# Three edits in a hybrid decoder step: mLSTM row operations at the second GLA value, SSD dt columns through one PSUM bank on ScalarE, urgent state updates, and a new step table

## The chip, the cores and the metric

The kernel runs on one core of a Trainium2 chip. The metric is the device time of one execution in microseconds (us); a measurement is the median over runs. The engines are TensorE (PE in the profile; its weight loads are PEld), VectorE (DVE), ScalarE (ACT), GpSimd (POOL) and SyncE (SP); each works through its own queue in order, and semaphores join them.

## The reference

One inference step of a small decoder trunk with two layers, for 512 prompt tokens and 8 samples of 4 tokens each (544 columns), model width 1024, all float32:

```python
for l in range(DEPTH):                      # DEPTH = 2
    if l % 2 == 0:                          # "AB": mLSTM heads and GLA heads
        mix, c, n, m, s = _ab_mixer(x, ...) # one input projection, 4 + 4 heads, one output projection
    else:                                   # "SSD": Mamba-2, 4 groups of 8 heads, causal conv of width 4
        mix, h, cv = _ssd_mixer(x, ...)
    x = _layernorm(DN_ALPHA * x + mix, ...)
    x = _layernorm(DN_ALPHA * x + _mlp(x, w1, w2), ...)   # squared ReLU, 4096 wide
```

In the mLSTM the gates give rows per head over the tokens: lf = log_sigmoid(f), its running sum b, and the running maximum m of b + (i - b), from which come the weights exp(D - m) of the scores. In the SSD, dt = softplus(dt_raw + bias), cs is the running sum of -exp(a_log) * dt in a chunk, and each group computes

```python
w = jnp.exp(seg) * dt                                  # seg[t, s] = cs[t] - cs[s], causal
y = einsum(CB, w, x) + einsum(C, h0) * exp(cs)
h = exp(cs_last) * h0 + einsum(exp(cs_last - cs) * dt, x, B)
```

for the prompt from a zero state, and for each sample from its given state. All new states are outputs.

## The kernel before

The work is in four stages: AB, MLP 0, SSD, MLP 1. Activations stand with features on the partitions, so a tile has 128 features x 272 columns (half of the 544; hf is the half). Each float32 weight tile is split on the chip into a high part whi (ScalarE, L167) and a rest wlo (VectorE, L168), and each product is three matmuls (xh by whi, xl by whi, xh by wlo; L378, L395, L590). These dense matmuls are the bulk of TensorE's work.

Everything else is fitted in between. Each of these side works (a GLA or mLSTM head, a group of the SSD, a LayerNorm) is a Python generator in a lane. `tick()` is called ahead of each dense matmul, and a lane whose count is used up goes on one step; `yield W["..."]` says how many dense matmuls are to pass until then, and `yield from need(key)` waits until another lane has set a key. So the table W fixes where TensorE's side instructions stand. A place in the program is given below as a tick: the number of dense matmuls ahead of it. The instructions of the other engines are put in order at build time by a scheduler, by when they could start in its model; code under `tc.high_priority()` is put ahead of what else is ready, and `tc.issue_after` (in `hold`) keeps operations behind a given one. On the chip each engine then follows its order strictly.

What the change touches:

- AB: `gla_scores` (L1050 to L1128) makes the scores of the GLA pairs q = 0 and 1 in levels: F = exp(A differences) on ScalarE, zq and zk on VectorE (L1092, L1094), gs on TensorE (L1102), a masked copy into sT (L1106). At its end "gscores" is set. `gla_heads` (L1390) runs the heads; ("g", n) is set when so many heads have given their values. A head ends in mean and variance (L873, L874), hf, hb and hn (L879 to L897).
- `ml_gates` (L1216): the mLSTM's rows on 4 partitions. First batch L1226 to L1237 (three passes on ScalarE, two scans and four passes on VectorE), second batch L1241 to L1258 behind head 2, then TensorE transposes uw into columns (uwt, L1280) and makes sample columns (sc, L1288).
- mLSTM heads: `ml_head` (row_bc's rowbc L769, md L1321, the outputs), pipelined with `W["mr"]` ticks between rounds (L1408); samples' products snum and supd (L969, L1008), for which GpSimd makes vm (L1004). When the heads are done, `then()` issues the loads of xf (L325) on GpSimd's queue.
- SSD: dt's rows (cs, dt, dw) are made on 32 partitions, written to DRAM for broadcast reads, and `dt_cols` (L1558) transposes them into two PSUM tiles rt and rt2, from which VectorE copies cols, ncs = -cs and csp. Each of four `group`s waits for "dt": transposes of B (Btp, Bts) and x (xt), the product cb, then per block of 128 tokens state, scores, outputs, each `W["sx"]` ticks on. E is loaded from DRAM, masked on GpSimd (L1666), exponentiated with ncs as bias (L1672), multiplied by cb (L1673). Then `samples`: four times `W["sq"]` ticks, products it (L1759) and sps (L1766), and eight updates h * dec + sp on VectorE (L1772), and after `W["so"]` ticks the output. All PSUM tiles by `pm` share a few banks, so a new one waits until the last reader of an older one is done.
- SSD's conv of the 24 tiles of x, B and C runs on ScalarE (L1604, L1609) and VectorE (L1606, L1611, L1612) as they come from the projection.
- `layernorm` (L455): sum over features (mu), squares, `W["v0"]` ticks later (first half; "v1" for the second, "vs" behind the SSD) their sum (var, L469), lnr, and xh and xl (L481, L482, L478) for the next stage.

Of the kernel before, what the change touches and what calls it, by code (L numbers as in the profile page):

```python
# [13 lines left out]
ALU = mybir.AluOpType  # L14
# [3 lines left out]
P = 128  # L18
D = 1024
KT = 8  # L20
NP = 512
NB, LS = 8, 4
NS = NB * LS
# [9 lines left out]
HEADM = 6  # L33
HEADA = 2

W = dict(dec=12, gates=30, gr=8, sc=16, lev=16, v=24, kd=10, out=48, hd=6, s0=42, ss=40, end=12, c0=20, u=13, s=16, ml=12, mr=52, dt=238, sg=72, sx=14, sq=26, so=48, l0=12, l1=12, v0=74, v1=55, f0=16, f1=18, f2=4, ls=20, vs=47)
GATES = ((0, 0, 4), (32, 4, 4), (64, 8, 16))
LEVELS = (64, 32, 16, 8, 4, 2, 1)

# [189 lines left out]
def trunk_kernel(ctx, tc, a, stages=("ab", "mlp0", "ssd", "mlp1")):  # L229
    nc = tc.nc  # L230
    V, S, G, TE = nc.vector, nc.scalar, nc.gpsimd, nc.tensor
# [6 lines left out]
    def pm(name):  # L238
        turn[0] += 1
        k = spare[0] and turn[0] % 5 == 0  # L240
        return psm.tile([P, 512], F32, tag="k" if k else "m", name=name, bufs=1 if k else 4)
# [10 lines left out]
    for st in stages:  # L252
# [10 lines left out]
        else:  # L263
# [3 lines left out]
            for kind, m, *r in MLP:  # L267
                if kind == "pair":
                    ws.plan(st, "pair", a["mlp_w1"][l, m], a["mlp_w1"][l, m + 1])
                else:  # L270
                    k, n = m % 8, r[0]
# [61 lines left out]
    def need(*keys):  # L333
        while not ready.issuperset(keys):
            yield 0
# [380 lines left out]
    def ab(pool, early, then):  # L716
# [11 lines left out]
        ident = C("ident")  # L728
# [486 lines left out]
        ml = {}  # L1215

        def ml_gates():
            rw = early.tile([P, T], F32, name="rw", bufs=1)
            uw = early.tile([P, T], F32, name="uw", bufs=1)
            z, t, b, u = rw[0:4], rw[32:36], rw[64:68], uw[0:4]  # L1220
            G.memset(uw, 0.0)
            S.copy(z, gate[32:36])
            S.copy(u, gate[0:4])
            yield from need("gscores")
            with hold("head"):
                S.activation(t, z, AF.Abs)  # L1226
                S.activation(t, t, AF.Exp, scale=-1.0)
# [11 lines left out]
            with hold("head"):  # L1239
                m = b  # L1240
# [37 lines left out]
            p = pm("uwt")  # L1278
            for b_ in range(4):
                TE.transpose(p[:, b_ * P:(b_ + 1) * P], uw[:, b_ * P:(b_ + 1) * P], ident)  # L1280
            cols = pool.tile([P, 4, 68], F32, name="cols", bufs=1)
# [4 lines left out]
            p = pm("sc")  # L1286
# [180 lines left out]
    def ssd(pool, ypool, dram, right, ahead, consts):  # L1467
# [7 lines left out]
        ident, smask, seqm, seye = C("ident"), C("smask"), C("seqm"), C("seye")  # L1475
# [81 lines left out]

        def dt_cols():  # L1558
            yield W["dt"]
            p1, p2 = pm("rt"), pm("rt2")  # L1560
            for b in range(4):
                TE.transpose(p1[:, b * 96:(b + 1) * 96], rows[:96, b * P:(b + 1) * P], ident[:96, :96])
            TE.transpose(p2[:NS, :96], rows[:96, NP:], ident[:96, :96])
            for o, b, q in ((slice(0, P), slice(0, 4), p1[:, :384].rearrange("p (b c) -> p b c", b=4)),
                            (slice(0, NS), slice(4, 5), p2[:NS, None, :96])):
                V.tensor_copy(cols[o, b], q[:, :, 32:])
                V.tensor_scalar(ncs[o, b], q[:, :, :32], -1.0, None, ALU.mult)
            V.tensor_copy(csp, p2[:NS, :32])
            for r in (64, 96):
                S.activation(ecs[r:r + NS], ncs[:NS, 4], AF.Exp, scale=-1.0)  # L1570
            ready.add("dt")
# [171 lines left out]
        def samples(g, X, outputs, z, Bs, Xs):  # L1743

            heads = slice(8 * g, 8 * g + 8)
            it = psm.tile([P, 512], F32, tag="k", name="it", bufs=1)
            for q in range(0, NB, 2):
                h0 = [pool.tile([P, 512], F32, tag="h0", name="h0", bufs=4) for _ in range(2)]
                for k in range(2):
                    nc.sync.dma_start(out=h0[k], in_=a["h0"][g, q + k])  # L1750
                hn = pool.tile([P, 2, 512], F32, tag="h0n", name="h0n", bufs=2)
                nc.sync.dma_start(out=hn, in_=a["h0n"][g, q // 2])
                Bm = pool.tile([96, 2, P], F32R, tag="Bm", name="Bm", bufs=2)
                for k in range(2):
                    S.activation(Bm[:, k], Bs.bitcast(F32), AF.Identity, scale=seqm[:96, q + k:q + k + 1])
                yield W["sq"]

                for k in range(2):
                    TE.matmul(it[64 + NS * k:64 + NS * k + NS], Cm[:, NS * (q + k):NS * (q + k) + NS], h0[k],  # L1759
                              start=q == 0, stop=q == NB - 2)  # L1760
                for i in range(2):
                    sp = pm("sps")
                    spv = sp.rearrange("p (j k n) -> p j k n", j=2, k=2)
                    for j in range(2):
                        m = 2 * i + j
                        TE.matmul(sp[:, 256 * j:256 * j + 256], Xs[:, m * P:(m + 1) * P], Bm.rearrange("p k n -> p (k n)"),  # L1766
                                  start=True, stop=True)
                    for j in range(2):
                        m = 2 * i + j
                        for k in range(2):  # L1770
                            h = hn[:, k, m * P:(m + 1) * P]
                            V.scalar_tensor_tensor(h, h, decs[:, 4 * g + m, q + k:q + k + 1], spv[:, j, k], ALU.mult, ALU.add)  # L1772
                nc.gpsimd.dma_start(out=a["s_h"][g, q // 2], in_=hn)
            V.tensor_tensor(z[64:].rearrange("p (h c) -> p h c", h=8), it[64:].rearrange("p (h c) -> p h c", h=8),
                            ecs[64:, heads, None].broadcast_to([64, 8, 64]), ALU.mult)
            yield W["so"]
            outputs(4)
            ready.add(("Y", g))
# [355 lines left out]
```

## Time and profile before

| | |
|---|---|
| runs (3) | 1504.7 us median, 1504.12 to 1508.48 |
| profiled execution | 1502.27 us, span 1500.6 |
| TensorE busy | 1468.2 us of the span, mean granted clock 0.993 |
| VectorE, ScalarE, GpSimd busy | 1100.2, 795.0, 192.8 us |

Durations come from the profiled execution, whose 1502.27 us consist of the span and 1.67 us around it. A row of a timeline gives start, length, engine, line, operation, out<-in, shapes, how many, and in brackets the idle time ahead and what ended it. DVEq, ACTq and PEq are issues by the engine's sequencer. In the changed kernel the lines behind L1560 have moved by one, those behind L1772 by two.

### The profile page before, as it was taken

The page shows a single profiled execution, that of the slowest core. Times are in us where ns is not written, and L with a number is a line of the kernel's source. Part 1 is how long each engine was busy: PE and PEld are TensorE (multiplying, and loading weights), DVE is VectorE, ACT ScalarE, POOL GpSimd, SP SyncE. Part 2 cuts the span into 40 slices and gives each one's busy share as a digit, 9 for nine tenths or more (in the row PEclk, how much of TensorE's full clock was granted, in tenths as well). Part 3 has the DMA queues.
Part 4 walks back from the last instruction along what each step waited for, and adds up shares of the span by engine and source line. Part 5 has one row for each costly group of instructions (what it writes and reads, how often), then busy time and mean ns, then how long its engine had stood idle before and what let it go on. Part 6 is the DMA issues. An engine that isn't in the chain of part 4 may idle for free.

```text
span 1500.6 us, 29204 instructions
## 1 busy us (share of the span) xinstructions
PE 1468.2 (98%) x11607; PEld 1419.1 (95%) x11607; DVE 1100.2 (73%) x2075; ACT 795.0 (53%) x1750; POOL 192.8 (13%) x228
## 2 busy tenths in 40 slices
PE   9998989999999999999999999999999999999997
PEld 8988989999999999999888789989999999999996
DVE  5675576786777667668999988777678677676656
ACT  7454457474444534537776675555247354444343
POOL 1410222100000000010243441421010000000000
PEclk9998999999999999999999999999999999999998
DMA  7211333413232332416657766365222333233221
GB/s 252 71 57 43 88 120 90 126 43 114 72 113 90 94 99 85 146 48 202 141 144 257 235 191 226 99 205 151 71 75 67 99 100 96 88 99 92 63 86 60
DMA packets 95025, 172.51 MB, mean 115 GB/s; under 512 B 15880, under 2 KB 50968, under 8 KB 94632
## 3 DMA queue, kind: packets, MB, share of 16 engines
q1 hardware_dynamic: 62280, 140.44, 30.3%
q10 hardware_dynamic: 29216, 17.19, 4.4%
q0 software_dynamic: 3392, 13.00, 2.3%
q8 instruction: 91, 1.49, 0.4%
q14 instruction: 46, 0.38, 0.1%
HBM read 153.48 MB, written 17.13 MB: 114 GB/s over the span
## 4 chain that ended last, share of the span: by engine, by line
PE 44%; DVE 5%; DMA 1%; issue 1%; ACT 1%; SPq 0%; DVEq 0%
PE psd L378 30%; PE psd L590 9%; PE yp L1712 1%; DVE wlo L168 1%; DVE acc L1606 1%; PE it L1759 1%; PE sp L1690 1%; PE ip L1687 1%; PE sps L1766 1%; DMA wraw<-mlp_w 0%; DVE h0n L1772 0%; PE xt L1651 0%; DMA ec<-d_ecs 0%; DVE xf L552 0%; DVE Y L1715 0%
## 5 line engine op out<-in xcount | busy, mean ns | idle before, releaser
L378 PE MATMUL psd<-xh,whi 128*128 128x272 f32 x1488 | 441.3, 297 | 1.0 <-ACT xh L287 1.0
L378 PE MATMUL psd<-xl,whi 128*128 128x272 f32 x1488 | 435.5, 293 | 1.3 <-DVE xl L478 1.3
L378 PE MATMUL psd<-xh,wlo 128*128 128x272 f32 x1488 | 435.7, 293 | 0.0
L378 PEld LDWEIGHTS psd<-xl,whi 128*128 128x128 f32 x1488 | 281.8, 190 | 7.9 <-issue 4.0
L378 PEld LDWEIGHTS psd<-xh,whi 128*128 128x128 f32 x1488 | 281.4, 189 | 8.0 <-issue 4.7
L378 PE MATMUL psd<-hh,whi 128*128 128x272 f32 x992 | 286.9, 289 | 0.0
L378 PE MATMUL psd<-hlo,whi 128*128 128x272 f32 x992 | 286.5, 289 | 0.0
L378 PE MATMUL psd<-hh,wlo 128*128 128x272 f32 x992 | 286.4, 289 | 0.0
L378 PEld LDWEIGHTS psd<-xh,wlo 128*128 128x128 f32 x1488 | 281.6, 189 | 4.4 <-issue 3.5
L168 DVE TENSOR_TENSOR wlo<-wraw,whi 128x1024 fp32r<-128x1024 f32 (+2 forms) x175 | 206.6, 1184 | 54.3 <-ACT whi L167 52.8
L167 ACT CAST whi<-wraw 128x1024 fp32r<-128x1024 f32 (+2 forms) x175 | 173.5, 997 | 130.2 <-PE psd L378 108.6
L378 PEld LDWEIGHTS psd<-hlo,whi 128*128 128x128 f32 x992 | 186.9, 188 | 0.2
L378 PEld LDWEIGHTS psd<-hh,whi 128*128 128x128 f32 x992 | 186.9, 188 | 0.2
L378 PEld LDWEIGHTS psd<-hh,wlo 128*128 128x128 f32 x992 | 186.9, 188 | 0.1
L428 DVE TENSOR_TENSOR xf<-xf,psd 128x272 f32<-128x272 f32 x208 | 88.4, 434 | 74.7 <-PE psd L378 74.2
L590 PE MATMUL psd<-xh,wlo 128*128 128x272 f32 x416 | 120.0, 289 | 0.0
L590 PE MATMUL psd<-xh,whi 128*128 128x272 f32 x416 | 119.9, 288 | 0.0
L590 PE MATMUL psd<-xl,whi 128*128 128x272 f32 x416 | 119.7, 288 | 0.0
L203 ACT CAST whi<-wsum 128x1024 fp32r<-128x1024 f32 x52 | 54.3, 1044 | 111.3 <-PE psd L590 70.2
L203 ACT CAST whi<-wraw 128x1024 fp32r<-128x1024 f32 (+1 forms) x52 | 43.4, 834 | 95.3 <-PE psd L378 84.2
L204 DVE TENSOR_TENSOR wlo<-wsum,whi 128x1024 fp32r<-128x1024 f32 x52 | 63.7, 1225 | 23.2 <-ACT whi L203 23.2
L590 PEld LDWEIGHTS psd<-xl,whi 128*128 128x128 f32 x416 | 78.5, 189 | 0.0
(488 smaller groups left out, 2836.4 us busy)
## 6 DMA issues: line engine op xcount, KB each, us to landing
wraw<-mlp_w SPq DMA_DIRECT2D x80, 512.0 KB, 3.7
wraw<-ssd_in SPq DMA_DIRECT2D x40, 512.0 KB, 3.8
wraw<-mlp_w SPq DMA_DIRECT2D x64, 256.0 KB, 3.0
wraw<-ab_in SPq DMA_DIRECT2D x22, 512.0 KB, 3.7
h<-h SPq DMA_DIRECT2D x32, 256.0 KB, 4.7
h0n<-h0n SPq DMA_DIRECT2D x16, 512.0 KB, 5.0
E<-d_cs ACTq DMA_DIRECT2D x16, 512.0 KB, 5.0
s_h<-h0n POOLq DMA_DIRECT2D x16, 512.0 KB, 4.0
```

The lines of the kernel that those rows point to most:

```text
L167: nc.scalar.copy(hi[:, r], w[:, r])
L168: nc.vector.tensor_tensor(lo[:, r], w[:, r], hi[:, r].bitcast(F32), ALU.subtract)
L203: self.cut[0] = nc.scalar.copy(hi, x).ins
L204: self.cut[1] = nc.vector.tensor_tensor(lo, x, hi.bitcast(F32), ALU.subtract).ins
L378: last[0] = TE.matmul(ps[:, :TH], (hi, hi, lo)[t][:, k, :], (rh, rl, rh)[t], start=i == 0, stop=i == n - 1).ins
L428: V.tensor_tensor(x, x, ps, ALU.add)
L590: last[0] = TE.matmul(ps, wt[:, k], bt[:, k], start=first and n == 0, stop=n == 11, skip_group_check=not first).ins
L1606: V.scalar_tensor_tensor(acc[:, :n], ci[:, w:w + n], cw[:, m, w:w + 1], acc[:, :n], ALU.mult, ALU.add)
L1687: TE.matmul(ip[:, j * P:(j + 1) * P], hT[:, j * P:(j + 1) * P], Cf[:, tk], start=True, stop=True)
L1690: TE.matmul(sp, Bt[:, b], xw, start=True, stop=True)
L1712: TE.matmul(ypv[64 * e:64 * e + 64, j], z[:, 64 * r:64 * r + 64], E[:, r], start=True, stop=True)
L1759: TE.matmul(it[64 + NS * k:64 + NS * k + NS], Cm[:, NS * (q + k):NS * (q + k) + NS], h0[k], start=q == 0, stop=q == NB - 2)
```

## The change

Three edits in the code, and new numbers in W:

- the first batch of `ml_gates` waits for ("g", 1), the second GLA value, not for "gscores"; the second batch waits for head 2 as before;
- `dt_cols` transposes all into one PSUM bank, and ScalarE empties it, urgent;
- the samples' state updates are urgent;
- W: the tick counts of 26 steps, of which `ml` has no effect (the pipeline takes its own gap).

```diff
--- before.py
+++ after.py
@@ -33,7 +33,7 @@
 HEADM = 6
 HEADA = 2
 
-W = dict(dec=12, gates=30, gr=8, sc=16, lev=16, v=24, kd=10, out=48, hd=6, s0=42, ss=40, end=12, c0=20, u=13, s=16, ml=12, mr=52, dt=238, sg=72, sx=14, sq=26, so=48, l0=12, l1=12, v0=74, v1=55, f0=16, f1=18, f2=4, ls=20, vs=47)
+W = dict(dec=11, gates=30, gr=11, sc=18, lev=16, v=21, kd=12, out=48, hd=5, s0=36, ss=40, end=10, c0=18, u=14, s=14, ml=9, mr=62, dt=258, sg=75, sx=12, sq=28, so=31, l0=13, l1=14, v0=86, v1=60, f0=18, f1=18, f2=3, ls=27, vs=36)
 GATES = ((0, 0, 4), (32, 4, 4), (64, 8, 16))
 LEVELS = (64, 32, 16, 8, 4, 2, 1)
 
@@ -1221,7 +1221,7 @@
             G.memset(uw, 0.0)
             S.copy(z, gate[32:36])
             S.copy(u, gate[0:4])
-            yield from need("gscores")
+            yield from need(("g", 1))
             with hold("head"):
                 S.activation(t, z, AF.Abs)
                 S.activation(t, t, AF.Exp, scale=-1.0)
@@ -1557,15 +1557,16 @@
 
         def dt_cols():
             yield W["dt"]
-            p1, p2 = pm("rt"), pm("rt2")
+            p = pm("rt")
             for b in range(4):
-                TE.transpose(p1[:, b * 96:(b + 1) * 96], rows[:96, b * P:(b + 1) * P], ident[:96, :96])
-            TE.transpose(p2[:NS, :96], rows[:96, NP:], ident[:96, :96])
-            for o, b, q in ((slice(0, P), slice(0, 4), p1[:, :384].rearrange("p (b c) -> p b c", b=4)),
-                            (slice(0, NS), slice(4, 5), p2[:NS, None, :96])):
-                V.tensor_copy(cols[o, b], q[:, :, 32:])
-                V.tensor_scalar(ncs[o, b], q[:, :, :32], -1.0, None, ALU.mult)
-            V.tensor_copy(csp, p2[:NS, :32])
+                TE.transpose(p[:, b * 96:(b + 1) * 96], rows[:96, b * P:(b + 1) * P], ident[:96, :96])
+            TE.transpose(p[:NS, 384:480], rows[:96, NP:], ident[:96, :96])
+            pv = p[:, :480].rearrange("p (b c) -> p b c", c=96)
+            with tc.high_priority():
+                for o, b in ((slice(0, P), slice(0, 4)), (slice(0, NS), slice(4, 5))):
+                    S.copy(cols[o, b], pv[o, b, 32:])
+                    S.mul(ncs[o, b], pv[o, b, :32], -1.0)
+                S.copy(csp, pv[:NS, 4, :32])
             for r in (64, 96):
                 S.activation(ecs[r:r + NS], ncs[:NS, 4], AF.Exp, scale=-1.0)
             ready.add("dt")
@@ -1769,7 +1770,8 @@
                         m = 2 * i + j
                         for k in range(2):
                             h = hn[:, k, m * P:(m + 1) * P]
-                            V.scalar_tensor_tensor(h, h, decs[:, 4 * g + m, q + k:q + k + 1], spv[:, j, k], ALU.mult, ALU.add)
+                            with tc.high_priority():
+                                V.scalar_tensor_tensor(h, h, decs[:, 4 * g + m, q + k:q + k + 1], spv[:, j, k], ALU.mult, ALU.add)
                 nc.gpsimd.dma_start(out=a["s_h"][g, q // 2], in_=hn)
             V.tensor_tensor(z[64:].rearrange("p (h c) -> p h c", h=8), it[64:].rearrange("p (h c) -> p h c", h=8),
                             ecs[64:, heads, None].broadcast_to([64, 8, 64]), ALU.mult)
```

TensorE has the same instructions in both kernels. What moves on the engines that TensorE waits for:

VectorE in AB before, from hb of GLA head 2 (hb belongs to its normalisation, rw and uw are the rows of `ml_gates`):

```order
L894 SCALAR_TENSOR_TENSOR hb<-bmv,hf 128x4
L168 TENSOR_TENSOR wlo<-wraw,whi 128x1024
L1185 TENSOR_TENSOR sst<-ss,prm 128x32
L1171 TENSOR_TENSOR szq<-sF,gq 128x32
L1167 TENSOR_TENSOR sF<-A 128x32
L1229 SCALAR_TENSOR_TENSOR rw<-rw 4x544
L1171 TENSOR_TENSOR szq<-sF,gq 128x32
L1173 SCALAR_TENSOR_TENSOR skz_470<-gk,con,sF 128x32 x2
L1230 SCALAR_TENSOR_TENSOR rw<-con,rw 4x544
L1167 TENSOR_TENSOR sF<-A 128x32
L873 BN_STATS bst<-num 128x6 x2
L1231 TENSOR_TENSOR uw<-uw,rw 4x544
```

VectorE in AB now: first among the levels of the second GLA pair's scores, then from the same hb on.

```order
L1106 COPY_PREDICATED sT<-con,gs 128x64x8
L1092 TENSOR_TENSOR zq<-F,qm 128x512
L1094 TENSOR_TENSOR zk_462<-gk,F 128x8x32
L1229 SCALAR_TENSOR_TENSOR rw<-rw 4x544
L1106 COPY_PREDICATED sT<-con,gs 128x32x16
L1092 TENSOR_TENSOR zq<-F,qm 128x512
L1094 TENSOR_TENSOR zk_464<-gk,F 128x4x64
L905 TENSOR_SCALAR cg<-hot,prm 128x512
L1230 SCALAR_TENSOR_TENSOR rw<-con,rw 4x544
L1120 TENSOR_TENSOR kd<-kd,gk 128x512
L1094 TENSOR_TENSOR zk_462<-gk,F 128x2x128
L1106 COPY_PREDICATED sT<-con,gs 128x16x32
```

```order
L894 SCALAR_TENSOR_TENSOR hb<-bmv,hf 128x4
L1241 TENSOR_TENSOR rw<-rw 4x544
L1250 TENSOR_SCALAR uw<-uw,rw 4x512
L1252 TENSOR_TENSOR uw<-uw,rw 4x32
L1258 TENSOR_SCALAR uw<-rw 4x544
L1261 TENSOR_TENSOR wi<-m_186,rw 4x32
L1271 TENSOR_TENSOR rw<-uw,con 4x128
L1244 COPY ms<-rw 4x8
```

The first batch (L1229, L1230, L1231, ...) has moved from behind hb into the levels of gla_scores, and behind hb the second batch (L1241 on) follows at once.

GpSimd before, near the last mLSTM heads (vm is what TensorE's supd multiplies, cg the gated head outputs, xf the residual's load):

```order
L917 TENSOR_TENSOR cg<-cg,gg 128x272
L917 TENSOR_TENSOR cg<-cg,gg 128x240
L325 DMA xf_2844<-xT 128x1088 x2
L325 DMA xf_2845<-xT 128x1088 x2
L1004 TENSOR_TENSOR vm<-vstk,con 128x390
L1004 TENSOR_TENSOR vm<-vstk,con 128x260
```

The same place now:

```order
L1004 TENSOR_TENSOR vm<-vstk,con 128x390 x2
L1004 TENSOR_TENSOR vm<-vstk,con 128x260
L917 TENSOR_TENSOR cg<-cg,gg 128x240
L917 TENSOR_TENSOR cg<-cg,gg 128x272
L325 DMA xf_2830<-xT 128x1088 x2
L325 DMA xf_2831<-xT 128x1088 x2
L917 TENSOR_TENSOR cg<-cg,gg 128x240
```

The xf loads stood ahead of the last two vm rows; they now stand behind all of them.

VectorE in the SSD before, in the samples of group 1 and the start of group 2 (h0n are the state updates, acc and Cf conv, zt the gate z):

```order
L1788 SCALAR_TENSOR_TENSOR zt<-zt,psd 128x272
L1606 SCALAR_TENSOR_TENSOR acc<-ci,sprm,acc 128x568 x2
L1772 SCALAR_TENSOR_TENSOR h0n<-h0n,decs,sps 128x128 x8
L168 TENSOR_TENSOR wlo<-wraw,whi 128x1024
L1788 SCALAR_TENSOR_TENSOR zt<-zt,psd 128x272
L1772 SCALAR_TENSOR_TENSOR h0n<-h0n,decs,sps 128x128 x3
L1611 SCALAR_TENSOR_TENSOR Cf<-Cf,acc 128x512
L1772 SCALAR_TENSOR_TENSOR h0n<-h0n,decs,sps 128x128
L1612 SCALAR_TENSOR_TENSOR Cf<-Cf,acc 128x32
L1772 SCALAR_TENSOR_TENSOR h0n<-h0n,decs,sps 128x128 x3
L1788 SCALAR_TENSOR_TENSOR zt<-zt,psd 128x272
L1772 SCALAR_TENSOR_TENSOR h0n<-h0n,decs,sps 128x128
```

The same place now:

```order
L1774 SCALAR_TENSOR_TENSOR h0n<-h0n,decs,sps 128x128 x8
L1607 SCALAR_TENSOR_TENSOR acc<-ci,sprm,acc 128x568
L168 TENSOR_TENSOR wlo<-wraw,whi 128x1024
L1774 SCALAR_TENSOR_TENSOR h0n<-h0n,decs,sps 128x128 x8
L1790 SCALAR_TENSOR_TENSOR zt<-zt,psd 128x272
L1612 SCALAR_TENSOR_TENSOR Cf<-Cf,acc 128x512
L1613 SCALAR_TENSOR_TENSOR Cf<-Cf,acc 128x32
L1790 SCALAR_TENSOR_TENSOR zt<-zt,psd 128x272
L1662 TENSOR_TENSOR z<-xt,scols 128x512
L1662 TENSOR_TENSOR xw<-xt,scols 128x512
L1739 TENSOR_TENSOR Bs<-Bt,Bs 32x128
L1674 TENSOR_TENSOR E<-E,cb 128x1024
```

The eight updates of a pair stand together, one batch ahead of zt and conv's Cf.

dt's columns before, on VectorE (scols is cols, Y the conv's output for x):

```order
L1611 SCALAR_TENSOR_TENSOR Cf<-Cf,acc 128x512
L1612 SCALAR_TENSOR_TENSOR Cf<-Cf,acc 128x32
L1566 COPY scols<-rt 128x256
L1611 SCALAR_TENSOR_TENSOR Y<-Y,acc 128x512
L1567 TENSOR_SCALAR ncs<-rt 128x128
L1612 SCALAR_TENSOR_TENSOR Y<-Y,acc 128x32
L1566 COPY scols<-rt_8860 32x64
L1567 TENSOR_SCALAR ncs<-rt_8860 32x32
L1568 COPY csp<-rt_8860 32x32
```

Now, on ScalarE:

```order
L1610 ACTIVATE Y<-acc 128x512
L1611 ACTIVATE Y<-acc 128x32
L1567 COPY scols<-rt 128x256
L1568 ACTIVATE ncs<-rt 128x128
L1567 COPY scols<-rt 32x64
L1568 ACTIVATE ncs<-rt 32x32
L1569 COPY csp<-rt 32x32
L1644 DMA E<-d_cs 128x8x128
L1629 COPY Bt<-Btp 128x512
L1571 ACTIVATE ecs<-ncs 32x32 x2
L1632 COPY Bt<-Bts 32x128
```

They have left VectorE and stand on ScalarE in one piece, ahead of the load of E and the copies of Bt. On TensorE rt is at tick 4950, before at 4930.

Some ticks of TensorE's side instructions, before and now: uwt 634 and 630; the last mLSTM head's hot transposes 977 and 1032; the SSD groups' starts 4930, 5198, 5460, 5916 and 4950, 5195, 5440, 5919; the outputs of the samples 5268, 5544, 5812, 6258 and 5267, 5512, 5757, 6235; var of the LayerNorm behind the SSD 7107 (first half) and 7257 (second), now 7120 and 7253, with the second half's mu at 7209 and now at 7216.

## Prediction

> **What bounds the kernel now.** I read the page's summary first, then the list of what TensorE waits for, then tables of 25 us stretches, and after that the instructions around each long wait. The head of the page:
>
> ```profile
> span 1500.6 us, 29204 instructions
> PE 1468.2 (98%) x11607; PEld 1419.1 (95%) x11607; DVE 1100.2 (73%) x2075; ACT 795.0 (53%) x1750; POOL 192.8 (13%) x228
> ```
>
> TensorE sets the time. 1500.6 - 1468.2 leaves 32.4 us in which it does nothing. An order change can only win those, plus what TensorE loses at a low clock. The instruction counts of TensorE are the same before and after. Next, the waits of TensorE by line (us in total, times, longest):
>
> ```profile
> PE uwt L1280 <- ACT uw L1254: 3.0, 1, 3.0
> PE gs L1102 <- DVE zk L1094: 2.7, 2, 2.0
> PE supd L1008 <- POOL vm L1004: 2.3, 2, 2.0
> PE xt L1651 <- DVE ncs L1567: 2.2, 1, 2.2
> PE yp L1712 <- DVE ec L1688: 1.8, 3, 0.8
> PE mkt L1367 <- ACT hn L897: 1.5, 1, 1.5
> PE rowbc L769 <- DVE E L1322: 1.4, 1, 1.4
> PE psd L378 <- DVE xl L478: 1.3, 1, 1.3
> PE cb L1653 <- DVE h0n L1772: 1.1, 2, 0.9
> PE sc L1288 <- DVE rw L1271: 0.9, 1, 0.9
> PE xt L1651 <- DVE h0n L1772: 0.9, 1, 0.9
> ```
>
> Uwt, gs, supd, mkt, rowbc and sc lie in the AB stage: 3.0 + 2.7 + 2.3 + 1.5 + 1.4 + 0.9 = 11.8 us. The lines from L1567 on, except xl, are SSD: 2.2 + 1.8 + 1.1 + 0.9 = 6.0 us. The stretches (length; busy us and instructions of PE, PEld, DVE, ACT, POOL; granted TensorE clock; the last two columns are DMA):
>
> ```profile
> 125.00:150.00 25.00, 21.02 (x145) 19.90 (x145) 16.72 (x52) 10.97 (x27) 2.15 (x3) 0.80 0.10 35
> 825.00:850.00 25.00, 22.49 (x174) 19.24 (x172) 24.90 (x45) 19.20 (x56) 11.46 (x11) 1.00 0.65 193
> 325.00:350.00 25.00, 25.00 (x201) 25.00 (x201) 20.16 (x29) 15.71 (x30) 0.00 (x0) 1.00 0.35 106
> 725.00:875.00 150.00, 143.68 (x1145) 125.04 (x1144) 144.14 (x246) 108.02 (x321) 61.02 (x66) 1.00 0.69 204
> ```
>
> The first stretch is the worst, and not through idle time alone: its clock is 0.80. The third shows dense work: 201 matmuls in 25 us, 0.125 us each, which is one tick of the planner. In the SSD stretch, the last row, VectorE (third pair) is busy 144.14 of 150 us, about as much as TensorE. Finer cuts behind the two longest AB waits, each beside a full-speed piece of like length:
>
> ```profile
> 134.70:144.90 10.20, 9.26 (x41) 8.53 (x39) 4.77 (x15) 4.23 (x12) 0.30 (x1) 0.51 0.15 53
> 146.00:156.20 10.20, 10.20 (x100) 9.88 (x100) 3.99 (x14) 5.35 (x13) 1.93 (x3) 1.00 0.25 66
> 223.45:226.90 3.45, 3.45 (x16) 3.26 (x16) 1.82 (x6) 0.82 (x3) 0.76 (x1) 0.53 0.78 319
> 227.00:230.45 3.45, 3.45 (x30) 3.45 (x30) 2.54 (x6) 2.55 (x5) 0.00 (x0) 1.00 0.62 169
> ```
>
> After the uwt wait TensorE ran 10.2 us at 0.51, and after the supd wait 3.45 us at 0.53, with 41 and 16 instructions where full speed did 100 and 30. So these two waits cost their length and half of what follows: 9.26 x 0.49 = 4.5 us and 3.45 x 0.47 = 1.6 us.
>
> **First row operations (need("g", 1)).** These rows are VectorE's and ScalarE's from the end of GLA head 2 to the uwt wait:
>
> ```profile
> 118.20 0.16 DVE L894 SCALAR_TENSOR_TENSOR hb<-bmv,hf 128x4 f32<-128x4 f32 x1 [0.76 <-ACT hf L880]
> 121.69 1.23 DVE L168 TENSOR_TENSOR wlo<-wraw,whi 128x1024 fp32r<-128x1024 f32 x1 [3.33 <-ACT whi L167]
> 123.37 0.72 DVE L1229 SCALAR_TENSOR_TENSOR rw<-rw 4x544 f32<-4x544 f32 x1
> 124.74 1.28 DVE L1230 TENSOR_TENSOR_SCAN rw<-con,rw 4x544 f32<-4x544 f32 x1
> 130.09 1.28 DVE L1237 TENSOR_TENSOR_SCAN rw<-rw 4x544 f32<-4x544 f32 x1
> 131.40 0.72 DVE L1241 TENSOR_TENSOR rw<-rw 4x544 f32<-4x544 f32 x1
> 132.15 1.11 DVE L1250 TENSOR_SCALAR uw<-uw,rw 4x512 f32<-4x512 f32 x1
> 133.50 0.66 ACT L1254 ACTIVATE uw<-uw 4x544 f32<-4x544 f32 x1 [0.70 <-DVE uw L1252]
> ```
>
> The chain to uw runs L1229 ... L1237, L1241, L1250, L1254, and ends at 134.16, when uwt starts. Changed, everything up to L1237 stands among the levels of GLA head 2's scores, and L1241 stands directly behind hb. From hb's end at 118.36 the rest takes 131.40 to 134.16, that is 2.8 us, so uw is there near 121.2. TensorE reaches uwt four dense matmuls earlier than before, about 130.7. That is some 9 us to spare: the 3.0 goes, the 0.9 of sc (the same chain, L1271) goes, and with the idle time goes its low clock, 4.5. What now carries the row work is GLA head 2: L1229, both scans and three small passes, by these rows about 5 us of VectorE, spread over levels whose operations are on the way to gs. In the trace VectorE is idle for 3.33 us ahead of 121.69, but not among the levels; so some of the gs wait stays. On the other side the weight casts no longer stand in front of zk and hb there: wlo is 1.23 in its row. Of 2.7 I keep 0.9 (bounds: 0, and 3.0 if all of the row work were in the way of one level); saved 1.8.
>
> **Wider head steps (mr 62, hd 5, end 10).** The supd wait has its reason in GpSimd's queue:
>
> ```profile
> 218.69 2.20 POOL L325 DMA_DIRECT2D xf<-xT  x4
> 220.90 1.42 POOL L1004 TENSOR_TENSOR vm<-vstk,con 128x390 f32<-128x390 f32 x2
> ```
>
> Vm, which TensorE wants, stands behind four issues of 2.20 us in all. In the changed order all vm products come before the xf loads. So the 2.3 goes to about 0.1, and the 1.6 of clock with it. The xf loads move later, and what reads them (the first residual, tick 1176, about 30 us on) covers this; without that cover they would cost up to 2.2 us. The mkt and rowbc waits (2.9) fall in a round where several steps meet at the same tick (818). With 62 ticks between heads, supd and the next head's scores stand 41 ticks apart instead of 18, and two bank reuses on hn fall away. At the round at 843 two banks are still freed by VectorE shortly before. I take 2.0 saved (bounds 0 and 2.9).
>
> AB: idle 3.9 + 1.8 + 2.2 + 2.0 = 9.9; clock 4.5 + 1.6 = 6.1; against that 1.0 for new small waits where steps now stand closer (s0, end, kd; bounds 0 and 2). Net -15.0.
>
> [...]
>
> **SSD.** The rows of dt's columns and of the state updates, and one operation that waits out a GpSimd operation beside it:
>
> ```profile
> 734.73 0.41 DVE L1566 COPY scols<-rt 128x256 f32<-128x256 f32 x1
> 735.66 0.28 DVE L1567 TENSOR_SCALAR ncs<-rt 128x128 f32<-128x128 f32 x1
> 736.19 0.17 DVE L1568 COPY csp<-rt 32x32 f32<-32x32 f32 x1
> 841.76 2.14 DVE L1772 SCALAR_TENSOR_TENSOR h0n<-h0n,decs,sps 128x128 f32<-128x128 f32 x8
> 771.19 1.84 DVE L1606 SCALAR_TENSOR_TENSOR acc<-ci,sprm,acc 128x568 f32<-128x568 f32 x1
> 768.42 4.00 POOL L1717 TENSOR_TENSOR Y<-Y,ec 128x512 f32<-128x512 f32 x1 [2.44 <-ACT whi L167]
> ```
>
> Xt waited 2.2 us because it reuses the bank of rt, which VectorE emptied between conv passes. Five evacuations of 0.2 to 0.4 us (1.2 us in all) go to ScalarE, which has 108.02 of 150 us in use. There they stand behind each other, and rt's bank goes to cb, four transposes further on. ScalarE's time for them is not in the trace; at VectorE's rates 1.2 us, less the 1.0 that Btp, Bts and xt take meanwhile, and up to 0.9 for a pass in progress. I take 0.7 of the 2.2 left: saved 1.5.
>
> The state updates, now urgent, are eight in a row behind their sps, so the banks that cb and xt wait for come free earlier: of 1.1 + 0.9 I leave 0.5, saved 1.5. What they are moved past is conv passes and, in places, wlo. The 1.8 of yp <- ec I leave as it is. Steps of 13 ticks instead of 15 give VectorE less time (three steps to a block: 6 ticks x 0.125 = 0.75 us), but by the order fewer weight splits fall into the two blocks between the three ec, one where there were three: 2 x 1.23 = 2.5 us less. For the backlog that this leaves I add 1.0. Bounds of the SSD term: -6.0 (all waits go) and +4. The second is 75 ticks (4950 to 5757 for three groups, before 4930 to 5812), 9.4 us, taken from VectorE's time, of which about half is conv and weight work that moves out with the ticks. Net -2.0.
>
> **LayerNorm (v0 86, vs 36).** Around the SSD's LayerNorm VectorE shows:
>
> ```profile
> 1120.76 1.32 DVE L478 SCALAR_TENSOR_TENSOR xl<-xf,lnp,xh 128x272 fp32r<-128x272 f32 x3
> 1122.73 2.62 DVE L461 SCALAR_TENSOR_TENSOR xf<-mu,xf 128x544 f32<-128x544 f32 x4 [0.65 <-PE mu L458]
> 1128.22 0.44 DVE L466 TENSOR_TENSOR lnq<-lnq 128x272 f32<-128x272 f32 x1
> ```
>
> The xl wait of 1.3 is there already. Var of the first half now comes 13 ticks (1.6 us) later, so xl does too, unless VectorE fills the time with work it had between: +0.8 (0 to 1.6). In the second half mu to L466 took 1122.73 to 1128.66, 5.9 us; var now stands 37 ticks (4.6 us) behind mu, not 48: +1.0 (0 to 1.4). The other two v0 places have 68 ticks (8.5 us) of cover behind var: 0 (to 0.5). Net +1.8.
>
> **Sum.** -15.0 - 2.0 + 1.8 = -15.2. The profiled execution took 1502.3 us (span 1500.6 and 1.7 around it): 1487.1. The median of the runs is 1504.7, 2.4 more, so the forecast is 1489.5. About 0.3%, 4.5 us, is what a measurement of this kernel can tell from no change.
>
> **Rivals.**
>
> *The waits go, others of 2 us come, and the clock falls again.* Row work of 5 us among head 2's levels makes gs wait 2 to 3 us once, and the low clock that costs 1.6 to 4.5 comes behind it. For it: a gs wait of 2.0 is there already, VectorE has no gap among those levels. Against: that wait brought no low clock. 1489.5 + 2 + 4.5 = 1496. Chance 0.18.
>
> *VectorE becomes the bound in the SSD.* The +4 end instead of -2: 1495.5. For it 144.14 of 150; against it that AB pays more than this. Chance 0.12.
>
> *The change does not do what it says:* the second batch (L1241 on) still waits for head 2's hb. If the row work in head 2's levels holds hb back by the 9 us to spare, uw is as late as before and 3.0 + 0.9 + 4.5 stay: 1497.9; with the LayerNorm's 1.6 + 1.4 and the SSD at 0 instead of -2, 1501 to 1502, no change. For it: hb already waits for ScalarE in its row. Against: 5 us of row work is less than 9. Chance 0.10.
>
> *Slower.* The urgent updates, 2.14 us per eight, stand ahead of wlo, and weights come too late for TensorE: 16 such batches, if each delays a dense matmul by its whole length, 34 us; 1489.5 + 34 = 1523. It decides where a split ends less than 2.1 us before its first matmul; below that, half of the batches already cost 17 us, 1506.5. Against it: no dense matmul of the SSD waits for wlo in the list above. Chance 0.05.
>
> **How the numbers follow.** The forecast's own case (1483 to 1494, by the bounds of gs, mkt and SSD) has 0.55, the rivals 0.18, 0.12, 0.10 and 0.05. Faster by over 0.3% (below 1500.2): 0.55 + 0.18 + 0.12, less 0.04 for their tails, 0.81; the same: most of the third and those tails, 0.13; slower 0.06. The range goes from 1482 to 1501: it takes in the first two rivals and half of the third.
>
> **What would show it.** Right: no uwt, sc, supd or mkt in the list of TensorE's waits, a clock of 1.0 in 125 to 150 us and 201 instructions there or near; xt <- rt gone and under 1 us on ScalarE's csp; a new var wait near 1120 us. Wrong: a stretch in the middle of the kernel at 0.5, gs waits over 2 us, dense matmuls waiting for wlo or for ci in 725 to 875 us.

## The result, and the profile after

The changed kernel takes 1485.0 us (median of four runs, 1484.6 to 1485.3) beside 1504.4 of the kernel before: ratio 0.9873, 95% interval 0.9842 to 0.9903. The forecast was 1489.5, range 1482 to 1501. The profiled executions are 1502.3 and 1484.6, so the working of the sum, -15.2, has to be set beside -17.7. The page of the changed kernel begins:

```profile
span 1482.9 us, 29204 instructions
PE 1461.2 (99%) x11607; PEld 1414.0 (95%) x11607; DVE 1093.6 (74%) x2070; ACT 794.8 (54%) x1755; POOL 180.5 (12%) x228
```

TensorE is idle for 21.7 us where it was 32.4, and its busy time is 7.0 us shorter with the same instructions. Most of that is clock: in the kernel before, TensorE was busy for 12.7 us in stretches at a granted clock of 0.50 (9.30 of the 10.24 us from 134.51 on, and all 3.41 from 223.26 on). At full clock this work would take 6.4 us less, an estimate: half of the 12.7. To see where, both traces are cut at two instructions that no edit moves, the first L395 of each MLP. The columns are those of the 25 us stretches. Before:

```profile
0.00:622.30 622.30, 607.96 (x4804) 594.51 (x4805) 428.98 (x879) 320.69 (x673) 67.69 (x86) 0.99 0.31 96
622.30:1438.10 815.80, 808.07 (x6407) 773.96 (x6406) 634.46 (x1124) 454.38 (x1037) 122.44 (x140) 1.00 0.44 133
1438.10:1500.60 62.50, 52.16 (x400) 50.60 (x398) 36.80 (x74) 19.93 (x42) 2.67 (x2) 0.94 0.17 62
```

After:

```profile
0.00:603.50 603.50, 600.65 (x4804) 589.03 (x4805) 425.04 (x879) 318.76 (x673) 66.38 (x86) 1.00 0.32 100
603.50:1419.90 816.40, 808.41 (x6408) 774.40 (x6407) 631.63 (x1119) 456.49 (x1042) 111.46 (x140) 1.00 0.43 133
1419.90:1482.90 63.00, 52.09 (x400) 50.59 (x398) 36.91 (x74) 19.57 (x42) 2.67 (x2) 0.94 0.17 61
```

All of the gain lies in the first part, with AB: -18.8 us, of which 14.3 - 2.9 = 11.5 are idle time and 7.3 busy time. The part with the SSD is 0.6 longer, the end 0.5. What TensorE still waits for in the changed kernel (us in total, times, longest):

```profile
PE var L469 <- DVE lnq L466: 1.4, 1, 1.4
PE psd L378 <- DVE xl L478: 1.3, 2, 0.9
PE cb L1654 <- DVE Cf L1612: 1.3, 1, 1.3
PE yp L1713 <- DVE h0n L1774: 1.3, 1, 1.3
PE yp L1713 <- ACT cb L1666: 1.0, 1, 1.0
PE gs L1102 <- DVE zk L1094: 0.8, 1, 0.8
PE mu L458 <- DVE lns L437: 0.7, 1, 0.7
PE sp L1691 <- DVE xw L1662: 0.6, 1, 0.6
PE mu L536 <- DVE xf L428: 0.5, 1, 0.5
```

Uwt, sc, supd, mkt and rowbc are gone. In the SSD the waits on ncs and ec are gone, 1.5 of the 2.0 on h0n are left (1.3 at yp, 0.2 at cb), and new are cb's wait for conv's Cf, yp's for cb and sp's for xw. The longest wait in the middle of the kernel is 1.4 us, and no stretch there runs below full clock (clock 1.00 in the first two of the rows after).

### The profile page after: what moved, and what is told of

It reads as the page before. It is cut to its first block, busy times and chain, and to the rows that moved or that the text cites. A ratio compares the mean times of both kernels' runs of the same rounds, so it can differ in the third digit from the quotient of the medians.

```text
span 1482.9 us, 29204 instructions
## 1 busy us (share of the span) xinstructions
PE 1461.2 (99%) x11607; PEld 1414.0 (95%) x11607; DVE 1093.6 (74%) x2070; ACT 794.8 (54%) x1755; POOL 180.5 (12%) x228
## 4 chain that ended last, share of the span: by engine, by line
PE 88%; DVE 7%; ACT 2%; issue 2%; DMA 1%; SPq 0%; DVEq 0%; ACTq 0%; POOLq 0%
PE psd L378 59%; PE psd L590 18%; DVE wlo L168 2%; PE yp L1713 1%; PE num L869 1%; DVE acc L1607 1%; PE it L1760 1%; PE sp L1691 1%; PE ip L1688 1%; PE sps L1767 1%; PE gs L1102 1%; DVE h0n L1774 1%; ACT whi L167 1%; DMA wraw<-mlp_w 1%; PE supd L1008 0%
## 5 line engine op out<-in xcount | busy, mean ns | idle before, releaser
L168 DVE TENSOR_TENSOR wlo<-wraw,whi 128x1024 fp32r<-128x1024 f32 (+2 forms) x175 | 209.6, 1202 | 46.0 <-ACT whi L167 45.6
```

The source lines that it names most:

```text
L168: nc.vector.tensor_tensor(lo[:, r], w[:, r], hi[:, r].bitcast(F32), ALU.subtract)
```

## Experiments

Each run has a label (e1 to e6 and e8 to e13), by which it is named further down. Of the table W the diffs show only the entries that change.

**The early row operations, taken back and alone.** First the changed kernel with this one line back:

```diff
-            yield from need(("g", 1))
+            yield from need("gscores")
```

> The changed kernel with one line back: the first row operations of the mLSTM gates wait for gscores again; all else, the step table too, stays as changed. Theory (the row work was late for uwt, and the idle time there brought the half clock): the waits uwt and sc come back with about 3.9 us and a stretch of some 10 us at a clock near 0.5 follows, 4.5 us: 1485.0 + 8.4 = 1493.4. Rival (the wider head steps alone give the row work its time): uwt waits under 1 us, no low clock, 1485 to 1487.

Measured (e1): 1496.1 (1491.2 to 1496.5), +11.0. Two of its waits, and the 3.41 us behind the uwt wait in the profiled execution, which is the fastest of the four:

```profile
PE uwt L1280 <- ACT uw L1254: 3.2, 1, 3.2
PE sc L1288 <- DVE rw L1271: 0.3, 1, 0.3
130.32:133.73 3.41, 3.41 (x16) 3.41 (x16) 3.20 (x11) 2.35 (x7) 0.00 (x0) 0.50 0.18 38
```

The theory holds: the wait is back, and the clock of 0.50 with it. The rival falls. In this execution the low clock there lasted 3.4 us and not 10; the other three took some 5 us more, and of them no trace was kept. The profiled one has a second fall of the clock, far behind, after var has waited 2.15 us at 1115 us (1.4 in the changed kernel; why it is longer here is open). Then the kernel before with the new line alone (the same diff the other way round, in the old table):

> The kernel before with this one line alone: the first row operations wait for the second GLA value; the old step table stays. Theory: uwt 3.0, sc 0.9 and the low clock of 4.5 go, the gs waits stay at 2.7 or grow by up to 1: 1504.5 - 8.4 = 1496, up to 1497. Rival (the row work among the levels is in the way of zk under the old table, and gs waits 2 to 3 us more, with or without low clock): 1499 to 1503.

Measured (e2): 1495.0 (1492.2 to 1496.4), -9.0 against the 1504.0 of the kernel before, taken beside it. Uwt is gone, and the row work is in the way of zk:

```profile
PE gs L1102 <- DVE zk L1094: 3.5, 2, 2.8
PE supd L1008 <- POOL vm L1004: 2.3, 2, 2.1
96.00:99.41 3.41, 3.41 (x16) 3.41 (x17) 3.21 (x4) 2.81 (x9) 1.98 (x2) 0.50 0.02 5
```

Gs has 0.8 more than before, the theory's end, but its longest wait is now 2.8, with 3.4 us at a clock of 0.50 behind it. So the gain of the line is right, and what the rival said of zk is true in part: 0.8 more and not 2 to 3, with low clock. A second fall, at 765 us, stands behind a wait of yp for ec that grew from 0.8 to 2.5.

**The other steps of AB.** The head steps back, all else as changed:

```diff
-hd=5, end=10, mr=62
+hd=6, end=12, mr=52
```

> The changed kernel with mr = 52, hd = 6 and end = 12, the old steps of the heads. Theory (the steps took away the supd, mkt and rowbc waits and the second low clock): these come back, 2.2 + 2.0 + 1.6 = 5.8: 1490.8, a stretch of some 3.4 us near 0.5 behind a supd wait. Rival (the supd wait went because the xf loads moved for another reason, the mkt and rowbc waits because TensorE comes earlier): at most 1487.

Measured (e3): 1489.1 (1488.9 to 1489.9), +4.1, between the two.

```profile
PE mkt L1367 <- ACT hn L897: 1.1, 1, 1.1
PE supd L1008 <- ACT vt L795: 0.6, 1, 0.6
PE supd L1008 <- POOL vm L1004: 0.4, 1, 0.4
```

Mkt is back with 1.1 of 1.5, rowbc is not in the list, and supd waits for GpSimd with 0.4 of 2.3 only: in this order xf loads stand ahead of vm products again, yet the wait is short. No low clock follows (mean granted clock 0.997, in the changed kernel 0.998). Next the rest of AB's steps:

```diff
-dec=11, gr=11, sc=18, v=21, kd=12, s0=36, c0=18, u=14, s=14
+dec=12, gr=8, sc=16, v=24, kd=10, s0=42, c0=20, u=13, s=16
```

> The changed kernel with the other steps of AB as before: dec = 12, gr = 8, sc = 16, v = 24, kd = 10, s0 = 42, c0 = 20, u = 13, s = 16; the early row operations and the head steps mr, hd and end stay changed. Theory (these carry the small rest: 19.4 - 9.0 for the early rows alone - 4.1 for the head steps - the SSD's and LayerNorm's shares leaves about 2): the gs waits come back in part, 1 to 2 us, 1486.5. Rival (they matter because head 2 comes too late without them: gs waits of 3 us and low clock): 1489 or more. Rival two (worth nothing): 1485 within 0.3.

Measured (e11): 1495.8 (1493.0 to 1498.5), +10.8. My theory of a small rest falls. Rival one is right in its time, and in its parts only half:

```profile
PE supd L1008 <- POOL vm L1004: 3.2, 1, 3.2
PE gs L1102 <- DVE zk L1094: 2.5, 2, 1.8
PE gs L1102 <- DVE rw L1234: 1.2, 1, 1.2
206.31:213.14 6.83, 5.59 (x19) 4.65 (x19) 1.72 (x5) 3.01 (x8) 2.56 (x4) 0.50 0.24 80
```

Gs waits 2.5 us for zk, no more than in the kernel before (2.7), and 1.2 for a row operation (rw L1234 is one). The larger part is supd: 3.2, and the 6.8 us of half clock, in which TensorE was busy for 5.6, cost 2.8 more. GpSimd's rows there:

```profile
206.00 0.70 POOL L917 TENSOR_TENSOR cg<-cg,gg 128x240 f32<-128x240 f32 x1 [8.31 <-DVE hf L893]
206.66 2.21 POOL L1004 TENSOR_TENSOR vm<-vstk,con 128x390 f32<-128x390 f32 x3
214.60 1.15 POOL L325 DMA_DIRECT2D xf<-xT  x2
```

This is not the wait of the kernel before: the xf loads stand behind vm. Vm stands behind a cg for which GpSimd waited 8.31 us on VectorE. Taken back one at a time, the three groups cost 11.0 + 4.1 + 10.8 = 25.9 us, more than the 19.4 that the whole change brings: they are not separate gains.

**dt's columns.** Two PSUM tiles and VectorE again, the new steps kept:

```diff
-            p = pm("rt")
+            p1, p2 = pm("rt"), pm("rt2")
...
-                    S.copy(cols[o, b], pv[o, b, 32:])
-                    S.mul(ncs[o, b], pv[o, b, :32], -1.0)
+                V.tensor_copy(cols[o, b], q[:, :, 32:])
+                V.tensor_scalar(ncs[o, b], q[:, :, :32], -1.0, None, ALU.mult)
```

> The changed kernel with dt's columns as before: two PSUM tiles, emptied by VectorE without urgency; the new steps stay. Theory (xt waited because the evacuations of rt stood between conv passes on VectorE): an xt wait of about 2 us behind ncs or csp returns, 1485.0 + 1.5 = 1486.5, and VectorE has 1.2 us more to do in the first block. Rival (the start of dt 20 ticks later is what took the wait away): no xt wait over 0.5 us, 1485 within 0.5.

Measured (e4): 1488.8 (1487.9 to 1491.6), +3.8.

```profile
PE cb L1653 <- DVE Cf L1611: 2.2, 1, 2.2
PE yp L1712 <- DVE ec L1688: 1.7, 2, 1.4
PE xt L1651 <- ACT Bt L1628: 0.6, 1, 0.6
```

The edit is worth 3.8, but not where I put it. No xt wait on ncs or csp comes back, which is the rival's result; its reason, the later start, is not shown. In this run the first xt (719.27 us) and cb (719.76) start before VectorE's first copy out of rt (719.88), so neither waited for rt's banks. In e6 below, with the old steps and the columns on ScalarE, no such wait is listed either: each of the two, the new steps and this edit, is enough without the other. What comes back are other waits on VectorE: on ec, and on Cf one that the changed kernel has with 1.3, here 2.2, with 3.4 us of half clock behind it. In the changed kernel the five copies are on ScalarE, the first, the second and the last in these rows:

```profile
717.97 0.37 ACT L1567 COPY scols<-rt 128x256 f32<-128x256 f32 x1 [0.32 <-PE rt L1563]
718.24 0.28 ACT L1568 ACTIVATE ncs<-rt 128x128 f32<-128x128 f32 x1
718.59 0.17 ACT L1569 COPY csp<-rt 32x32 f32<-32x32 f32 x1
```

They take 0.8 us from start to end, and cb, which was to take rt's bank, starts right behind them, at 718.81, with no wait in the list.

**The urgent updates and the SSD's steps.** The updates not urgent:

```diff
-                            with tc.high_priority():
-                                V.scalar_tensor_tensor(h, h, decs[...], spv[:, j, k], ALU.mult, ALU.add)
+                            V.scalar_tensor_tensor(h, h, decs[...], spv[:, j, k], ALU.mult, ALU.add)
```

> The changed kernel with the samples' state updates not urgent; all else stays. Theory (urgent updates free the banks of sps earlier): waits of cb, xt or yp on h0n return with 1.5 to 2 us in all instead of the 1.5 that are left (1.3 yp, 0.2 cb), so +0.5: 1485.5. Rival (urgent updates push conv and cb back and make the yp and cb waits that the changed kernel shows, 1.3 + 1.3 + 1.0): those go, 1482 to 1484.

Measured (e5): 1485.5 (1484.7 to 1486.6), +0.5 with overlapping runs. Waits on h0n are 1.2 + 0.5 + 0.4 = 2.1 where the changed kernel has 1.3 + 0.2 = 1.5:

```profile
PE yp L1713 <- DVE h0n L1773: 1.2, 1, 1.2
PE xt L1652 <- DVE h0n L1773: 0.5, 1, 0.5
PE cb L1654 <- DVE h0n L1773: 0.4, 1, 0.4
```

In the direction of the theory, too small to be sure of. Of the rival's three waits, cb for Cf and yp for cb are gone, but cb now waits 1.0 for Y, and sp 0.5 more for xw, so nothing is won. Then the SSD's old steps, with both code edits kept:

```diff
-dt=258, sg=75, sx=12, sq=28, so=31
+dt=238, sg=72, sx=14, sq=26, so=48
```

> The changed kernel with the old steps of the SSD: dt = 238, sg = 72, sx = 14, sq = 26, so = 48; columns on ScalarE and urgent updates stay. Theory (the steps are worth little, the waits go with the two edits in the code): 1485 within 1.5, waits of the SSD of 3 to 5 us in all. Rival one (denser steps make VectorE late, so the old ones are better): 1481 to 1483, fewer yp waits. Rival two (the later start of dt is what took the xt wait): an xt or cb wait of about 2 us near the start of the SSD, 1487.

Measured (e6): 1485.9, with single runs at 1484.4, 1485.9, 1485.9 and, the profiled one, 1490.3. In the median the steps are worth 0.9, as the theory has it. In the profiled run, the slowest, the SSD's waits on the list are 2.1 + 2.0 + 1.0 + 0.7 = 5.8 and not 3 to 5, and the two longest have 3.4 us of half clock behind them each:

```profile
PE sp L1691 <- ACT cb L1666: 2.1, 1, 2.1
PE sps L1767 <- ACT Cf L1611: 2.0, 1, 2.0
```

The changed kernel has no wait of this length there. Whether the other three runs had such falls is not recorded. Rival two is not borne out: the wait at sp stands at 799 us, 84 us behind rt, and no xt wait is listed.

**The LayerNorm's distances.**

```diff
-v0=86, vs=36
+v0=74, vs=47
```

> The changed kernel with v0 = 74 and vs = 47, the old distances of the variance in the LayerNorms. Theory (vs = 36 makes var wait 1.4 us for the squares, v0 = 86 delays xl behind the SSD): both are lost time, 1485.0 - 1.4 = 1483.6, with psd waiting for xl about as before (1.3). Rival (the chain to xl of the second half is what matters, and the time won at var is lost again at xl or at mu): 1485 within 0.5.

Measured (e8): 1483.6 (1483.0 to 1484.5). The var wait is gone, psd on xl stands at 1.4 against 1.3, as the theory has it. The mu wait of 0.7 at the start of the SSD is gone too. So these two numbers of the table together are a loss of 1.5. I ran it once more (e13) beside the changed kernel itself (e12):

> The changed kernel itself once more, beside the next one on the same chip: 1485.0 within 0.5, and a spread under 1 us, since no gap in the middle of it is as long as 1.5 us and none can cost clock.

> The changed kernel with v0 = 74 and vs = 47 once more, beside the changed kernel on the same chip. Theory (the 1.4 us wait of var is lost time): 1.4 below it, 1483.6. Rival (the first difference was the chip's or the day's): within 0.5 of it.

Measured: the changed kernel 1485.2 (1484.6 to 1485.4), this one 1483.7, 1.6 below, with runs at 1483.0, 1483.3, 1484.0 and 1486.9. The last is above all runs of the changed kernel, and its cause is open. This version beats both kernels in the median: 0.9864 of the kernel before (0.9844 to 0.9884).

**The clock.** Some equal waits brought half clock and others none. In the kernel before, gs waited 1.96 us up to 95.17 without a fall and supd 2.04 us up to 221.81 with one; var's wait of 2.15 brought a fall in e1 and none in e6 and e11. The length of the stretch was 3.4, 6.8 or 10.2 us. To see what sorts them, gaps of chosen length were put into MLP 0 of the changed kernel, at eight places between its blocks (the calls in the loop over the blocks, and the tile gt, are not shown):

```diff
+    def gap(n):
+        p, t = pm("gap"), gt
+        TE.matmul(p[:, :P], ones, ones, start=True, stop=True)
+        with tc.high_priority():
+            S.copy(t, p[:, :4])
+            for _ in range(n):
+                S.copy(t, t)
+        p = pm("gap")
+        TE.matmul(p[:, :4], ones, t, start=True, stop=True)
```

> The changed kernel with eight idle gaps of TensorE put into MLP 0, between its blocks: TensorE makes one small product, ScalarE copies it and copies it over 3, 6, 9, 12, 5, 8, 15 and 20 times, and TensorE waits for the last copy; gaps of about 1 to 4 us. Nothing of the computation is left out. Theory (the granted clock falls where a fixed, free-running stretch of time has had too little work, so a gap's length alone does not decide): gaps under 1 us bring none, gaps of 3.4 us and more all bring a stretch at 0.5, those between some do and some not, and the stretches last 3.4 us or a multiple. Rival (a fixed length decides, about 2.5 to 3 us): gaps sort by length without overlap, and every stretch has the same length.

Measured (e9): the gaps were 1.53, 1.61, 2.89, 3.56, 1.98, 2.66, 4.25 and 5.38 us. The clock fell after 2.66, 3.56, 4.25 and 5.38, and not after 2.89. Length alone does not sort them. The four falls come at 436.76, 491.38, 518.68 and 549.40 us: the last three lie 16.00, 24.00 and 33.00 times 3.41333 us behind the first. The second kernel has equal gaps:

> As the first kernel with idle gaps in MLP 0, now with 10 copies five times and 14 three times: five gaps of one length, about 2.9 us, and three of about 4 us, at other places in time. Nothing of the computation is left out. Theory (a free-running grid of 3.41 us; the clock falls at a grid point when more than some 1.9 us of the 3.41 before it were idle): equal gaps come out differently, by where the grid cuts them; all falls of one run lie a multiple of 3.413 us apart; 4 us always falls. Rival (length alone): the five equal gaps all fall or none does.

In this run (e10) the first five gaps were 3.11 us four times and 3.33 once. Three of them, by the row of the product that waits:

```profile
372.86 0.59 PE L594 MATMUL gap<-gapt,ones 128*128 128x4 f32 x2 [3.11 <-ACT gapt L592]
418.25 0.38 PE L594 MATMUL gap<-gapt,ones 128*128 128x4 f32 x2 [3.11 <-ACT gapt L592]
473.88 0.39 PE L594 MATMUL gap<-gapt,ones 128*128 128x4 f32 x2 [3.11 <-ACT gapt L592]
```

and the clock (third number from the end) in the 3.41 us that begin at the grid point in or behind each:

```profile
372.44:375.85 3.41, 2.99 (x13) 2.99 (x14) 0.00 (x0) 0.33 (x2) 0.00 (x0) 0.50 0.00 0
416.81:420.22 3.41, 1.98 (x16) 1.98 (x17) 1.88 (x3) 1.19 (x7) 0.00 (x0) 1.00 0.11 22
474.84:478.25 3.41, 3.41 (x18) 3.41 (x17) 0.00 (x0) 0.39 (x1) 0.00 (x0) 0.50 0.23 88
```

Gaps of 3.11 us, one with the clock's fall in its last half microsecond, one with nothing, one with a fall a microsecond after it: the rival falls. The other two of the five brought a fall as well. All seven falls behind the gaps of this run lie whole multiples of 3.41333 us apart, within 0.002 of a whole number, and so do the two falls in the middle of the kernel before (134.51 and 223.25, 26.00 apart). The gap at 418.25 was cut by the grid point at 416.81 into 1.67 and 1.44 us.

In these traces the falls go by the idle time in one window of the grid, not by one gap. An eighth fall of e10, at 877.61 us in the SSD, stands on the same grid behind two waits of 0.80 and 1.36 us in one window. Over all traces, as long as the kernel still has work for TensorE, falls came where at least 1.92 us of one 3.41 us window were idle (1.92 in e11, ahead of the fall at 206.31), and none where it was at most 1.75 (at var in e6); at the end of e12 the clock fell behind a window with 1.79. This sorts the equal waits above: the window held 1.62 us of idle time at gs and 1.96 at supd, and at var 1.95 in e1, 1.75 in e6 and 1.31 in e11.

## Why the prediction was right, and where its sizes were off

- **Row operations.** Uwt, sc and their clock went, as said; gs kept 0.8 and 0.2 against 0.9. The row work stands among the levels as the order showed:

```profile
96.78 0.72 DVE L1229 SCALAR_TENSOR_TENSOR rw<-rw 4x544 f32<-4x544 f32 x1
99.96 1.28 DVE L1230 TENSOR_TENSOR_SCAN rw<-con,rw 4x544 f32<-4x544 f32 x1
```

  That this is cheap is not the line's own doing: under the old steps of AB the gs waits grew from 2.7 to 3.5 (alone, e2) or to 2.5 + 1.2 (with the new head steps, e11). Two readings behind my 0.9 were wrong, so that it came so close is in part luck. VectorE did have idle time among those levels in the kernel before:

```profile
90.82 1.23 DVE L168 TENSOR_TENSOR wlo<-wraw,whi 128x1024 fp32r<-128x1024 f32 x1 [1.49 <-ACT whi L167]
93.99 0.69 DVE L1092 TENSOR_TENSOR zq<-F,qm 128x512 f32<-128x512 f32 x1 [1.25 <-ACT F L1087]
```

  And in the changed kernel wlo still stands among the levels: at 91.67 us, for 2.06 us, ahead of a zq. The runs put the small gs wait on the steps as a whole; which of the nine numbers of e11 does it was not tried.
- **Head steps.** Supd's wait went to 0, and GpSimd's order is as said, all vm products ahead of the xf loads. But the loads are not the whole reason: in e3 they stand ahead of vm's last products again and supd waits 0.4, and in e11 they stand behind vm and supd waits 3.2. Mkt and rowbc went whole, 2.9, where I took 2.0, and vtr (0.3) and the first xh (0.4 less; this one varies between 0.2 and 1.1 from run to run) came on top. The share of the head steps by themselves is 4.1 and not 5.8.
- **New small waits, +1.0.** They did not come. AB was forecast at -15.0 and gave -18.8: 0.9 from mkt and rowbc, 1.0 here, 0.7 from vtr and xh, and the rest, about 1.2, is busy time: 7.3 us against my 6.1 for the clock. Half of the 12.7 us that TensorE was busy in the two slow stretches is 6.4; where the other 0.9 went is open.
- **SSD, -2.0.** The waits went from 6.4 (sps's 0.4 with them) to 1.3 + 1.3 + 1.0 + 0.6 + 0.2 = 4.4: -2.0, as forecast, but with the wrong parts, so this agreement is luck. The ec waits that I left at 1.8 went, and new ones on Cf and cb came. VectorE did not become the bound: 140.5 busy us of 150 (725 to 875), and e6 puts the steps at 0.9 in the median.
- **LayerNorm, +1.8.** Var waits 1.4 (I took 1.0, bound 1.4). Xl is unchanged at 1.3, where I took +0.8. A mu wait of 0.7 at the start of the SSD was missed; it goes with the old numbers (e8), so one of the other two v0 places, taken as free, was not. Also missed was 0.5 at the last mu, whose cause is open. e8 shows v0 and vs as a loss of 1.5, as said. All in all the parts behind AB were forecast at -0.2 and gave +1.1 (0.6 and 0.5).
- **The forecast's offset.** I carried the profile's distance to the median (2.4 us) over. In fact the changed kernel's profile lies 0.4 below its median: the medians differ by 19.4, the profiles by 17.7. In the kernel before the most idle time that any 3.41 us hold is 1.96 at gs, 2.04 at supd and 2.22 at xt; on the grid of the profiled run it was 1.62, 1.96 and 1.39, and of these only supd had a fall behind it. So by the figures above where the grid lies can decide at these gaps, and its time scatters (1499.3 to 1508.5 in the first four runs); in the changed kernel no stretch of 3.41 us between the start and the end holds more than 1.42 us of idle time, wherever the grid lies, and it holds 1484.6 to 1485.4 in eight runs. That its scatter comes from the clock fits e1, e6 and the means of the clock (its 1501.2 us run has 0.996, its 1506.4 us run 0.989), but only the profiled runs show the falls themselves.

The rival of new 2 us waits with low clock did not happen in the changed kernel, but e2 is just that, and e11 with supd in the place of gs: it was one table away. Urgent updates ahead of wlo (the slower rival) cost nothing that shows. The steps l0, l1, v1, f0, f2 and ls, which the new table also changes, were not taken back; their share is not known.

## What to carry to other kernels

Price idle time of TensorE by its length and by the clock behind it. Up to 1.75 us within one 3.41 us window (e6) it cost only itself here, and two waits of 0.80 and 1.36 us in one window together had a fall behind them (e10). From 1.92 us on (e11; once, at the end of e12, at 1.79) it cost up to 1.7 us more for each window at a clock of 0.50, an estimate: half of 3.41. Where the window's edges lie changed between executions of one kernel: the fall at the end came at 1475.5 us in e8 and at 1473.2 in e13, 2.3 us and so no whole window apart. In the changed kernel the scatter of the times went with the long waits; that the clock made it fits the runs, but is not shown run by run. Steps that fill the same engines' time are to be taken back in groups: three groups cost 25.9 us when each was undone alone, more than the 19.4 of the whole change. And look at what a shared table moves besides its purpose: two LayerNorm numbers in it lost 1.5 us.

## What the runs showed of the hardware that was not expected

- In each trace all falls of the clock stand at points of a grid of 3.41333 us that runs on through the whole execution (26.00 steps between two falls of the kernel before, 289.00 in e1). The falls went by the idle time in the window before: a fall came at 1.92 us (e11) and more (at 1.79 at the end of e12), none at 1.75 (e6) and less.
- How long the slow stretch lasted went with the windows that followed, but the limit is open. In e9 and e10 it was one window where the next one was idle for at most 0.1 us, and two where it was idle for 0.4 us or more: 3.4 us after the 2.66 gap (0.09 idle behind the fall), 6.8 after the 3.56 gap (0.69). In the kernel before it was three, with 0.29 and 0.65 us idle in the first two. Yet at the start of e1 and e4 the clock rose behind a window with 0.5 us idle.
- VectorE's passes out of PSUM of 0.41, 0.28 and 0.17 us in the kernel before took 0.37, 0.28 and 0.17 on ScalarE in the changed one (scols, ncs and csp out of rt).
